# Two feed-forward layers, most gate/value products by Strassen's seven-product block form, the second matrix in four rounds

## The chip, the cores and the metric

The kernel runs on one core of a Trainium2 chip. The metric is device time in microseconds (us) from launch to the last output; smaller is better. Before the change three runs took 1251.07, 1249.19 and 1251.08 us, so the median is 1251.07.

The engines are named as in the profile: PE multiplies matrices, PEld loads its weights, DVE, ACT and POOL work elementwise, SP issues the transfers (DMA). Sums of products are formed in PSUM, everything else is kept in SBUF, both with 128 partitions.

## The reference

The trunk has two layers over 512 tokens of 1024 channels. Each layer is a mixer (layer 0: gated short convolution and attention; layer 1: a convolution module) and then a SwiGLU feed-forward, each between two norms and added to the stream. The change is in the feed-forward and in the norm behind it:

```python
def rms_norm(x, g):
    y = xf * lax.rsqrt(jnp.mean(xf * xf, axis=-1, keepdims=True) + RMS_EPS)
    return y * g
def swiglu_ffn(h, w_ffn_in, w_ffn_out):
    g, u = jnp.split(h @ w_ffn_in, 2, axis=-1)      # (512,1024) @ (1024, 2*2816)
    return (jax.nn.silu(g) * u) @ w_ffn_out         # (512,2816) @ (2816,1024)
...
for layer in range(2):
    ...                                             # mixer
    f = swiglu_ffn(rms_norm(h, norm_ffn_pre[layer]), w_ffn_in[layer], w_ffn_out[layer])
    h = h + rms_norm(f, norm_ffn_post[layer])
```

## The kernel before

Channels lie on partitions, tokens on the free axis: a tile is 128 channels by 512 tokens, and the stream is `NK` = 8 such tiles. Every float32 product is carried by three passes over operands that are split as v = H + L (`mm3`, lines 188 to 193: `wh` by `xh`, `wh` by `xl`, `wl` by `xh`). A weight block is 128 by 128, and 8 of them make one chunk of 512 KB. `ensure` streams the chunks in the order in which they are used: SP loads one into a raw buffer (`wr`, 2 of them), ACT copies it, rounded, into `wh` (line 173), DVE subtracts that from the raw chunk into `wl` (line 175; POOL for a few chunks outside the feed-forward). `wh` and `wl` have 5 buffers each. `take` asks for two chunks beyond the one in use.

The inner dimension 2816 of the feed-forward is 22 tiles. One *pair* is the gate tile and the value tile of the same 128 inner channels: 2 x 8 blocks x 3 passes = 48 matmuls of 512 columns (`pairs`). `glu_evict` then takes both sums out of PSUM: DVE multiplies each by `R`, the per-token factor of the norm (lines 783, 785), ACT does the Silu of the gate (784), DVE multiplies the two (786), and the result is split by ACT (`gh`, 787) and DVE (`gl`, 788). It lies in numbered slots `z`.

Each feed-forward is done in two halves of 11 pairs. Pairs 0 and 1 of the first are made in `cross`, in token halves, while the norm ahead is still being finished. After pairs 2 to 10 the first half's second product follows: `rows` makes 8 output tiles (`m`) of 11 k steps each, 33 matmuls of 512 columns a tile. Six of these partial sums go to SBUF (`KEPT`), the two others are put back into PSUM later by matmuls with an identity (lines 718 to 720). Then come pairs 11 to 21 and the second half's product: `WIDE` = 5 whole tiles, and the last three in token halves (`half_rows`), so that the norm behind them can begin on one half. `Boundary` adds the partial sums, normalises and adds to the stream.

PE runs its instructions in the order in which the program writes them. For DVE, ACT, POOL and SP a scheduler lays out the order when the program is built; each engine then works strictly along its own queue, so an instruction that has to wait holds up all that are queued behind it.

## Time and profile before

| | before |
|---|---|
| median of three runs, us | 1251.07 (1249.19 to 1251.08) |
| span of the profiled execution, us | 1248.6 |
| PE busy, us (share of the span) | 1185.8 (95%) |
| weight loads on PE, us | 1005.8 (81%) |
| DVE busy, us | 735.6 (59%) |
| ACT busy, us | 490.0 (39%) |
| POOL busy, us | 265.0 (21%) |
| mean granted TensorE clock (1.00 is full speed) | 0.978 |

The profiled execution is listed with its span alone, from the first to the last instruction, 2.5 us under the median of the runs. Shares are means over the whole span. The two feed-forwards are stages of their own in it (about 243 to 655 us and 842 to 1230 us), in which the engines are used quite differently from the rest; the profile's table of 40 slices and its windows show that. Idle time of an engine is listed with its releaser, the event that ended it.

### The profile page before, as it was taken

Reading aid. Unit: us, or ns where it says so; the run is one execution under the profiler, and the core shown is the slowest. Engines: PE = TensorE matmul, PEld = TensorE weight load, DVE = VectorE, ACT = ScalarE, POOL = GpSimd, SP = SyncE. Lnnn points to the kernel's source line nnn. Section 1 sums busy time; section 2 is a strip of 40 time slices with the busy share of each in tenths; the row PEclk is TensorE's granted clock in tenths of the full one; section 3 lists DMA queues with packets and bytes.
Section 4 is the critical chain, followed back from the end, with each engine's and each line's share of the span. In section 5 each row is a group of like instructions: output and inputs, shape, how many; then the busy total and the mean of one; then the engine's idle time right before and its main releaser. Section 6 shows DMA issues by size and latency. Waiting matters only on the chain.

```text
span 1248.6 us, 15995 instructions
## 1 busy us (share of the span) xinstructions
PE 1185.8 (95%) x6134; PEld 1005.8 (81%) x6134; DVE 735.6 (59%) x1266; ACT 490.0 (39%) x862; POOL 265.0 (21%) x268
## 2 busy tenths in 40 slices
PE   8899999989999999999988998898999999999996
PEld 6677677888888888888887897898888888888885
DVE  7578985496443234443398999948844422444425
ACT  4366664534332222332244575464332322332220
POOL 4132322460000000001475359124300000000021
PEclk9999999999999999999989999898999999999998
DMA  5332223313233233223221543123133233233212
GB/s 177 113 106 85 85 68 102 119 51 99 89 100 102 87 99 101 94 92 102 92 71 52 168 131 97 28 68 102 51 101 101 88 98 99 89 101 102 90 46 68
DMA packets 43116, 115.86 MB, mean 93 GB/s; under 512 B 4696, under 2 KB 14040, under 8 KB 43040
## 3 DMA queue, kind: packets, MB, share of 16 engines
q1 hardware_dynamic: 39936, 109.30, 28.1%
q10 hardware_dynamic: 2384, 3.15, 0.8%
q0 software_dynamic: 720, 2.39, 0.6%
q8 instruction: 48, 0.79, 0.3%
q14 instruction: 28, 0.23, 0.1%
HBM read 109.05 MB, written 5.78 MB: 92 GB/s over the span
## 4 chain that ended last, share of the span: by engine, by line
PE 73%; DVE 17%; DMA 4%; ACT 2%; issue 2%; POOL 1%; SPq 0%; ACTq 0%; DVEq 0%; POOLq 0%
PE pg L191 22%; PE pg L193 22%; PE pg L192 22%; DVE xl L675 2%; DVE h L672 2%; DVE wl L175 2%; DVE tb L663 2%; PE pg L737 1%; DVE st_u L281 1%; POOL acc L234 1%; PE ps L298 1%; PE pg L734 1%; DMA wr<-w_fi 1%; PE pg L735 1%; PE pp L541 1%
## 5 line engine op out<-in xcount | busy, mean ns | idle before, releaser
L191 PE MATMUL pg<-xh,wh 128*128 128x512 f32 (+1 forms) x960 | 372.1, 388 | 0.2 <-DVE z L459 0.2
L193 PE MATMUL pg<-xh,wl 128*128 128x512 f32 (+1 forms) x960 | 368.4, 384 | 2.0 <-DVE wl L175 2.0
L192 PE MATMUL pg<-xl,wh 128*128 128x512 f32 (+1 forms) x960 | 367.8, 383 | 2.0 <-DVE xl L331 2.0
L173 ACT ACTIVATE wh<-wr 128x1024 fp32r<-128x1024 f32 (+1 forms) x186 | 193.3, 1040 | 424.3 <-PE pg L192 349.9
L175 DVE TENSOR_TENSOR wl<-wr,wh 128x1024 fp32r<-128x1024 f32 (+1 forms) x157 | 192.3, 1226 | 168.2 <-ACT wh L173 168.1
L234 POOL TENSOR_TENSOR acc<-acc,sq 128x256 f32<-128x256 f32 x70 | 63.7, 925 | 749.5 <-ACT sq L241 746.5
L193 PEld LDWEIGHTS pg<-xh,wl 128*128 128x128 f32 x960 | 181.1, 189 | 38.8 <-DVE wl L175 3.0
L192 PEld LDWEIGHTS pg<-xl,wh 128*128 128x128 f32 x960 | 181.4, 189 | 36.6 <-DVE xl L331 2.8
L191 PEld LDWEIGHTS pg<-xh,wh 128*128 128x128 f32 x960 | 181.6, 189 | 33.9 <-issue 0.7
L191 PE MATMUL pg<-z,wh 128*128 128x512 f32 (+1 forms) x514 | 183.2, 357 | 0.0
L192 PE MATMUL pg<-z,wh 128*128 128x512 f32 (+1 forms) x514 | 182.1, 354 | 1.1 <-DVE z L391 1.1
L193 PE MATMUL pg<-z,wl 128*128 128x512 f32 (+1 forms) x514 | 182.1, 354 | 0.0
L192 PEld LDWEIGHTS pg<-z,wh 128*128 128x128 f32 x514 | 97.9, 190 | 15.9 <-DVE z L391 1.5
L191 PEld LDWEIGHTS pg<-z,wh 128*128 128x128 f32 x514 | 97.9, 190 | 14.7 <-ACT m L651 0.3
L193 PEld LDWEIGHTS pg<-z,wl 128*128 128x128 f32 x514 | 97.9, 190 | 14.4
L785 DVE TENSOR_TENSOR t<-pg,R 128x512 f32<-128x512 f32 (+1 forms) x48 | 31.0, 645 | 126.9 <-PE pg L193 126.7
L175 POOL TENSOR_TENSOR wl<-wr,wh 128x1024 fp32r<-128x1024 f32 x29 | 71.8, 2476 | 125.4 <-ACT wh L173 113.8
L783 DVE TENSOR_TENSOR t<-pg,R 128x512 f32<-128x512 f32 (+1 forms) x48 | 31.0, 646 | 86.7 <-PE pg L193 83.0
L918 DVE SCALAR_TENSOR_TENSOR ps<-z,vecs,ps 128x512 f32<-128x512 f32 x69 | 47.7, 747 | 0.1
L674 ACT ACTIVATE xh<-h,vecs 128x256 fp32r<-128x256 f32 x48 | 23.4, 506 | 58.4 <-DVE h L672 58.4
L734 PE MATMUL pg<-xh,wh 128*128 128x256 f32 x160 | 44.9, 305 | 1.2 <-ACT xh L1082 1.2
L735 PE MATMUL pg<-xh,wl 128*128 128x256 f32 x160 | 44.3, 301 | 0.0
(250 smaller groups left out, 1526.2 us busy)
## 6 DMA issues: line engine op xcount, KB each, us to landing
wr<-w_fi SPq DMA_DIRECT2D x88, 512.0 KB
wr<-w_fo SPq DMA_DIRECT2D x44, 512.0 KB
wr<-w_p SPq DMA_DIRECT2D x24, 512.0 KB
wr<-w_in SPq DMA_DIRECT2D x16, 512.0 KB
wr<-w_out SPq DMA_DIRECT2D x8, 512.0 KB
h<-x SPq DMA_DIRECT2D x8, 256.0 KB
wr<-w_xa SPq DMA_DIRECT2D x8, 256.0 KB
wr<-w_v SPq DMA_DIRECT2D x4, 512.0 KB
```

What stands on the lines that cost most here:

```text
L173: act(h[:, cs], raw[:, cs], AF.Copy)
L175: eng.tensor_tensor(out=l[:, cs], in0=raw[:, cs], in1=h[:, cs], op=ALU.subtract)
L191: mm(ps, wh, xh, start=first, stop=False)
L192: mm(ps, wh, xl, start=False, stop=False)
L193: mm(ps, wl, xh, start=False, stop=last)
L234: eng.tensor_tensor(out=acc, in0=acc, in1=t, op=ALU.add)
L663: stt(out=t, in0=self.s[k][:, cs], scalar=col(self.gpost + k), in1=rp, op0=ALU.mult, op1=ALU.mult)
L734: mm(ps, wh, xt[0][k][:, cs], start=k == 0 and m % 2 == 0, stop=False)
L735: mm(ps, wl, xt[0][k][:, cs], start=False, stop=False)
L783: tt(out=tg, in0=pg, in1=R[:, cs], op=ALU.mult)
L785: tt(out=tu, in0=pu, in1=R[:, cs], op=ALU.mult)
L918: stt(out=a if j < n - 1 else res, in0=u[:, j : j + T], scalar=w_col(i, j), in1=a, op0=ALU.mult, op1=ALU.add)
```

## The change

Of each feed-forward's 22 pairs, 0 to 3 stay as they are (`CLASSIC`). Pairs 4 to 21 are made by Strassen's form in Winograd's variant. The pair is read as a 2x2 block product: the gate matrix over the value matrix, each cut into two halves of the 1024 input channels (`a11 a12` over `a21 a22`), times the tokens' input, cut into channel halves and token halves (`b11 b12` over `b21 b22`). Seven products replace eight; each has 4 k steps x 3 passes of 256 columns. For them

- `combine` loads both weight chunks and builds `s1`, `s3`, `s2` (POOL) and `s4` (DVE) from them, and splits seven quarter-pair blocks into 4 + 4 buffers; the last split's subtract is POOL's;
- `strassen_x` and `strassen_last` build sums `t1` to `t4` of the tokens' input once a layer, on POOL, DVE and ACT;
- `strassen` runs the seven products, takes each out of PSUM and puts the sums together: ACT copies two, DVE combines five of 256 columns, POOL makes two steps of 512 (`tu` and the product with `R`).

The 22 inner tiles are worked in four rounds of 5, 6, 5, 6 pairs (`ROUNDS`), each followed by its part of the second product into 8 partial sums in SBUF: the first round copies them there, the others add to them on DVE. `WIDE` goes from 5 to 2, and the identity matmuls go. The second matrix's chunks are cut across output tiles, with 2 or 3 DMAs each, and are split by ACT and DVE. The value side isn't multiplied by `R` any more; the norm behind the feed-forward gets an epsilon per token for that.

The diff, cut to its core (line numbers in the text on the changed kernel are those of the changed file):

```diff
+ROUNDS = ((0, 5), (5, 11), (11, 16), (16, 22))
+CLASSIC = 4
-WIDE = 5
-KEPT = 6
+WIDE = 2
...
         def add_ffn(l):
-            for hf in range(2):
-                for i in range(HALF):
-                    for s in range(2):
-                        add("fi", w_fi[:, l, hf * HALF + i, s], s if (hf, i) == (0, 0) else None)
-                for c in range(HALF):
-                    add("fo", w_fo[:, l, hf, c])
+            for p0, p1 in ROUNDS:
+                for p in range(p0, p1):
...
+                        add("fs", (w_fi[:, l, p, 0], w_fi[:, l, p, 1]))
...
+                for c in range(n):
...
+                    add("fo", parts)
...
+                if name == "fo":
+                    r3 = raw.rearrange("p (a b) -> p a b", a=8)
+                    for lo, hi, part in ap:
+                        nc.sync.dma_start(r3[:, lo:hi], part)
+                    act(h, raw, AF.Copy)
+                    tt(out=l, in0=raw, in1=h, op=ALU.subtract)
...
+        def combine(top, bottom):
+            i = combined[0]
+            combined[0] += 1
+            a1 = alloc("wr", (P, D), F32, 2)
+            a2 = alloc(("pth", "ptl")[i % 2], (P, 2560), F32)
+            s4 = slot(12 + i % 2, dt=F32)
+            nc.sync.dma_start(a2[:, :D], bottom)
+            nc.sync.dma_start(a1, top)
+            hs, ls = ([alloc(n, (P, D), FR, 5) for _ in range(4)] for n in ("wh", "wl"))
+            pool = nc.gpsimd.tensor_tensor
+
+            def half(i, src, eng=nc.vector):
+                n = src.shape[1]
+                act(hs[i][:, :n], src, AF.Copy)
+                eng.tensor_tensor(out=ls[i][:, :n], in0=src, in1=hs[i][:, :n], op=ALU.subtract)
...
+            pool(out=s1, in0=a2[:, :T], in1=a2[:, T:D], op=ALU.add)
+            half(0, a1)
+            pool(out=s32.rearrange("p (a b) -> p a b", a=2),
+                 in0=a2[:, : 2 * D].rearrange("p (a b) -> p a b", a=2)[:, :, :T],
+                 in1=a1[:, :T].unsqueeze(1).to_broadcast([P, 2, T]), op=ALU.add)
+            half(1, a2[:, T : D + T])
+            half(2, s32)
+            tt(out=s4, in0=s2, in1=a1[:, T:], op=ALU.add)
+            half(3, s4, nc.gpsimd)
...
+        def strassen_x(bd, gpre):
...
+                pool(out=t1, in0=a[:, HT:], in1=a[:, :HT], op=ALU.subtract)
+                tt(out=t2, in0=b[:, HT:], in1=t1, op=ALU.subtract)
...
+        def strassen(xs, R, g, p):
+            w = take("fs", 1)[0]
+            def product(a, b):
+                ps = psum("g")[:, :HT]
+                for j in range(4):
+                    js = slice(j * P, (j + 1) * P)
+                    mm3(ps, (w[a][0][:, js], w[a][1][:, js]), xs[j][b], j == 0, j == 3)
+                return ps
...
+            act(p1, product("a11", "b11"), AF.Copy)
+            act(p5, product("s1", "t1"), AF.Copy)
+            tt(out=u23[:, lo], in0=product("s2", "t2"), in1=p1, op=ALU.subtract)
+            tt(out=tg[:, lo], in0=product("a12", "b21"), in1=p1, op=ALU.add)
+            tt(out=u23[:, hi], in0=product("s3", "t3"), in1=u23[:, lo], op=ALU.add)
+            nc.gpsimd.tensor_tensor(out=tu.rearrange("p (a b) -> p a b", a=2),
+                                    in0=u23.rearrange("p (a b) -> p a b", a=2),
+                                    in1=p5.unsqueeze(1).to_broadcast([P, 2, HT]), op=ALU.add)
+            tt(out=tg[:, hi], in0=product("s4", "b22"), in1=tu[:, lo], op=ALU.subtract)
+            nc.gpsimd.tensor_tensor(out=tg, in0=tg, in1=R, op=ALU.mult)
+            act(tg, tg, AF.Silu)
+            tt(out=tu[:, lo], in0=product("a22", "t4"), in1=u23[:, hi], op=ALU.add)
+            tt(out=tu, in0=tu, in1=tg, op=ALU.mult)
+            act(gh, tu, AF.Copy)
+            tt(out=gl, in0=tu, in1=gh, op=ALU.subtract)
...
+            def more(m, ps, c0, cn):
+                tt(out=part[m], in0=ps, in1=part[m], op=ALU.add)
+
+            for r, (p0, p1) in enumerate(ROUNDS):
+                weave(chain(*(strassen(xs, pre.R, g, p) for p in range(max(p0, CLASSIC), p1))))
+                st, rhs = Stream("fo"), [g[i][1:] for i in range(p1 - p0)]
+                if r < len(ROUNDS) - 1:
+                    weave(rows(st, p1 - p0, rhs, range(NK), more if r else first))
```

What that does to the queues is seen at three places. Names carry a buffer number; `z` slots hold `gh` and `gl`, `sq` and `sqp` the first two products, `acc` the pair of sums `u23`, `pth` and `ptl` the value chunk and its sums, in turn.

DVE's queue in the middle of a half, one pair before the change:

```order
L783 TENSOR_TENSOR t_653_3139<-pg_646_3081,R_490_2060 128x512
L175 TENSOR_TENSOR wl_661_3180<-wr_659_3178,wh_660_3179 128x1024
L785 TENSOR_TENSOR t_654_3140<-pg_650_3112,R_490_2060 128x512
L786 TENSOR_TENSOR t_654_3140<-t_654_3140,t_653_3139 128x512
L175 TENSOR_TENSOR wl_669_3221<-wr_667_3219,wh_668_3220 128x1024
L788 TENSOR_TENSOR z11_652_3138<-t_654_3140,z10_651_3137 128x512
```

The same engine after, one pair in the middle of the second round:

```order
L913 TENSOR_TENSOR acc_812_3838<-pg_817_3869,sq_813_3839 128x256
L929 TENSOR_TENSOR z5_784_3700<-t_786_3702,z4_783_3699 128x512
L915 TENSOR_TENSOR t_810_3836<-pg_818_3883,sq_813_3839 128x256
L218 TENSOR_TENSOR wl_805_3820<-ptl_798_3811,wh_801_3816 128x1024
L917 TENSOR_TENSOR acc_812_3838<-pg_819_3897,acc_812_3838 128x256
L229 TENSOR_TENSOR z12_824_3947<-pth_823_3946,wr_822_3945 128x512
L218 TENSOR_TENSOR wl_806_3821<-ptl_798_3811,wh_802_3817 128x1024
L922 TENSOR_TENSOR t_810_3836<-pg_820_3912,t_811_3837 128x256
L926 TENSOR_TENSOR t_811_3837<-pg_821_3928,acc_812_3838 128x256
L218 TENSOR_TENSOR wl_829_3954<-wr_822_3945,wh_825_3950 128x1024
L927 TENSOR_TENSOR t_811_3837<-t_811_3837,t_810_3836 128x512
```

Six instructions have become eleven: three weight splits instead of two, one sum of weights (229), and five evictions of 256 columns for two of 512.

POOL's queue before has nothing between the last square of the norm ahead of the first feed-forward and the sums of the norm behind it:

```order
L234 TENSOR_TENSOR acc_526_2338<-acc_526_2338,sqp_570_2624 128x256
L247 TENSOR_TENSOR sqp_572_2632<-h6_464_2026 128x256
L247 TENSOR_TENSOR sqp_574_2640<-h7_465_2027 128x256
L234 TENSOR_TENSOR acc_526_2338<-acc_526_2338,sqp_572_2632 128x256
L234 TENSOR_TENSOR acc_924_4723<-acc_924_4723,sq_929_4767 128x256
```

After, there are five instructions for each of the 18 pairs; for the pair shown above they are

```order
L222 TENSOR_TENSOR pth_823_3946<-pth_823_3946 128x512
L224 TENSOR_TENSOR pth_823_3946<-pth_823_3946,wr_822_3945 128x1024
L918 TENSOR_TENSOR t_811_3837<-acc_812_3838,sqp_814_3840 128x512
L218 TENSOR_TENSOR wl_807_3822<-z13_799_3812,wh_803_3818 128x512
L923 TENSOR_TENSOR t_810_3836<-t_810_3836,R_490_2060 128x512
```

The first two already work for the pair after the next (`pth_823`), the fourth for the next one (`wl_807`).

ACT's queue where the first half's pairs end and the second product begins, before:

```order
L784 ACTIVATE t_713_3499<-t_713_3499 128x512
L173 ACTIVATE wh_734_3581<-wr_733_3580 128x1024
L787 ACTIVATE z20_711_3497<-t_714_3500 128x512
L173 ACTIVATE wh_738_3613<-wr_737_3612 128x1024
L802 ACTIVATE m0_715_3507<-pg_725_3517 128x512
```

The same engine where the second round ends, after:

```order
L928 ACTIVATE z8_833_3969<-t_836_3972 128x512
L185 ACTIVATE wh_866_4200<-wr_865_4199 128x1024
L185 ACTIVATE wh_869_4207<-wr_868_4206 128x1024
L185 ACTIVATE wh_873_4240<-wr_872_4239 128x1024
L924 ACTIVATE t_852_4089<-t_852_4089 128x512
L185 ACTIVATE wh_877_4273<-wr_876_4272 128x1024
L928 ACTIVATE z10_850_4087<-t_853_4090 128x512
```

Before, the last pair's Silu (784) has one chunk of the second matrix between itself and `gh` (787). Now three chunks (185) stand ahead of the last pair's Silu (924) and a fourth between it and `gh` (928).

## Rows read from the trace of the kernel before

**Rows 1.** The page: POOL's busy time, and its tenths in 40 slices of the span.

```profile
PE 1185.8 (95%) x6134; PEld 1005.8 (81%) x6134; DVE 735.6 (59%) x1266; ACT 490.0 (39%) x862; POOL 265.0 (21%) x268
...
POOL 4132322460000000001475359124300000000021
```

**Rows 2.** Windows (from:to length, busy us by engine, clock, DMA share, GB/s).

```profile
core 0: us, PE busy (x) PEld busy (x) DVE busy (x) ACT busy (x) POOL busy (x), PEclk, DMA share, GB/s
300.00:430.00 130.00, 130.00 (x569) 106.52 (x568) 51.28 (x58) 39.10 (x47) 0.00 (x0) 1.00 0.31 97
```

**Rows 3.** Timeline of PE (start, length of one) in a pair, 26 steps apart.

```profile
319.83 0.39 PE L192 MATMUL pg<-xl,wh 128*128 128x512 f32 x1
...
325.73 0.39 PE L191 MATMUL pg<-xh,wh 128*128 128x512 f32 x1
```

**Rows 4.** Timeline of PE in second products: 31 steps, then 55 of 256 columns.

```profile
395.70 0.40 PE L192 MATMUL pg<-z,wh 128*128 128x512 f32 x1
...
402.95 0.39 PE L193 MATMUL pg<-z,wl 128*128 128x512 f32 x1
...
1209.31 0.28 PE L191 MATMUL pg<-z,wh 128*128 128x256 f32 x1
...
1215.85 0.28 PE L192 MATMUL pg<-z,wh 128*128 128x256 f32 x1
```

**Rows 5.** Timeline of DVE: the same instruction in two pairs that follow each other.

```profile
355.85 0.69 DVE L783 TENSOR_TENSOR t<-pg,R 128x512 f32<-128x512 f32 x1 [2.22 <-PE pg L193]
...
366.73 0.69 DVE L783 TENSOR_TENSOR t<-pg,R 128x512 f32<-128x512 f32 x1 [2.21 <-PE pg L193]
```

**Rows 6.** Groups by form (busy us, mean ns of one, idle before and releasers).

```profile
L175 DVE TENSOR_TENSOR wl<-wr,wh 128x1024 fp32r<-128x1024 f32 x149 | 185.8, 1248 | 168.2 <-ACT wh L173 168.1
L788 DVE TENSOR_TENSOR z<-t,z 128x512 fp32r<-128x512 f32 x40 | 27.4, 685 | 0.7 <-ACT z L787 0.7
L783 DVE TENSOR_TENSOR t<-pg,R 128x256 f32<-128x256 f32 x8 | 3.4, 419 | 3.7 <-ACT R L683 3.6
L173 ACT ACTIVATE wh<-wr 128x1024 fp32r<-128x1024 f32 x178 | 188.4, 1059 | 424.2 <-PE pg L192 349.9 <-issue 34.5 <-DMA wr<-w_v 11.1
L784 ACT ACTIVATE t<-t 128x512 f32<-128x512 f32 x40 | 25.3, 632 | 0.1
L175 POOL TENSOR_TENSOR wl<-wr,wh 128x1024 fp32r<-128x1024 f32 x29 | 71.8, 2476 | 125.4 <-ACT wh L173 113.8 <-DVE ps L918 7.0 <-PE pp L256 4.6
L881 POOL TENSOR_TENSOR z<-z,z 128x512 f32<-128x512 f32 x15 | 17.7, 1202 | 0.0
```

**Rows 7.** Timeline of POOL and DVE where both work at once.

```profile
160.83 2.40 POOL L175 TENSOR_TENSOR wl<-wr,wh 128x1024 fp32r<-128x1024 f32 x1 [7.71 <-ACT wh L173]
160.98 0.35 DVE L524 SCALAR_TENSOR_TENSOR h<-h,ccol,ps 128x128 f32<-128x128 f32 x1 [0.17 <-PE ps L520]
...
161.50 2.27 DVE L388 TENSOR_TENSOR t<-t,m 128x512 f32<-128x512 f32 x1
...
243.99 1.22 DVE L175 TENSOR_TENSOR wl<-wr,wh 128x1024 fp32r<-128x1024 f32 x1 [1.41 <-ACT wh L173]
...
244.31 1.51 POOL L234 TENSOR_TENSOR acc<-acc,sq 128x256 f32<-128x256 f32 x1 [8.48 <-ACT sq L241]
...
253.00 0.92 POOL L234 TENSOR_TENSOR acc<-acc,sq 128x256 f32<-128x256 f32 x1
253.24 1.76 DVE L175 TENSOR_TENSOR wl<-wr,wh 128x1024 fp32r<-128x1024 f32 x1
```

**Rows 8.** The chain of waits: transfers of whole chunks on it (start, length).

```profile
830.05 5.05 DMA wr<-w_p
...
837.47 3.42 DMA wr<-w_fi
```

**Rows 9.** Windows after a wait of PE (columns as in the second group).

```profile
664.00:667.00 3.00, 0.00 (x0) 0.00 (x0) 2.89 (x8) 0.00 (x0) 2.55 (x4) 1.00 0.00 0
667.00:670.00 3.00, 2.80 (x13) 2.80 (x14) 1.24 (x4) 1.52 (x2) 0.00 (x0) 0.52 0.00 0
670.00:673.00 3.00, 3.00 (x19) 2.76 (x19) 1.89 (x4) 2.46 (x7) 1.36 (x1) 0.91 0.00 0
```

More of the change, by code (lines that the diff above doesn't have):

```diff
@@ L157, in ensure @@
                 name, ap, spare = chunks[len(split)]
+                if name == "fs":
+                    split.append((name, combine(*ap), None))
+                    continue
                 count[name] = count.get(name, -1) + 1
@@ L289, in rsqrt_cols @@
             b = alloc("st_b", (P, 4), F32, 3)[:, :n]
+            if not isinstance(eps, float):
+                stt(out=a, in0=sums, scalar=scale, in1=eps, op0=ALU.mult, op1=ALU.add)
+                ts(out=b, in0=a, scalar1=-0.5, scalar2=None, op0=ALU.mult)
+                return newton(a, b, n)
             ts(out=a, in0=sums, scalar1=scale, scalar2=eps, op0=ALU.mult, op1=ALU.add)
@@ L627, in trunk, with __init__ @@
         class Boundary:
[L630 removed]
+            def __init__(self, gpost, gpre, bias=None, kept=(), before=None):
+                self.before, self.eps = before, {}
                 self.gpost, self.gpre, self.bias = gpost, gpre, bias
@@ L653, in post0 @@
             def post0(self, hf):
-                self.cols[hf] = rsqrt_cols(self.sums.cols(hf), 2, 1.0 / D, RMS_EPS)
+                eps = RMS_EPS if self.before is None else self.before.eps[hf]
+                self.cols[hf] = rsqrt_cols(self.sums.cols(hf), 2, 1.0 / D, eps)
             def post1(self, hf):
@@ L679, in pre0 @@
             def pre0(self, hf):
-                self.cols[hf] = rsqrt_cols(self.pre.cols(hf), 2, 1.0 / D, RMS_EPS)
+                sums = self.pre.cols(hf)
+                self.cols[hf] = rsqrt_cols(sums, 2, 1.0 / D, RMS_EPS)
+                self.eps[hf] = alloc(f"st_eps{hf}", (P, 4), F32)[:, :2]
+                ts(out=self.eps[hf], in0=sums, scalar1=RMS_EPS / D, scalar2=RMS_EPS * RMS_EPS, op0=ALU.mult, op1=ALU.add)
             def pre1(self, hf):
@@ L707, in rows, with half_rows @@
                     yield
-        def half_rows(st, nk, rhs, ms, hf, evict, base=0, back={}):
+        def half_rows(st, nk, rhs, ms, hf, evict, base=0):
             cs = slice(hf * HT, (hf + 1) * HT)
@@ L715, in half_rows @@
                     mm3(ps, st[(m - base) * nk + k], (rhs[k][0][:, cs], rhs[k][1][:, cs]),
-                        k == 0, k == nk - 1 and m not in back)
+                        k == 0, k == nk - 1)
                     if k == nk - 1:
-                        if m in back:
-                            for j in range(2):
-                                mm(ps, eye, back[m][j][:, cs], start=False, stop=j == 1)
                         evict(m, ps, hf * HT, HT)
@@ L772, in cross, with glu_room @@
             return [(LATE0[n], bd.steps("pre0", 1)), (LATE1[n], lambda: ready(1))]
+        def glu_room(g, p):
+            i = p - max(r[0] for r in ROUNDS if r[0] <= p)
+            if i not in g or g[i][0] != p:
+                g[i] = (p, slot(2 * i), slot(2 * i + 1))
+            return g[i][1:]
         def glu_evict(g):
@@ L792, in ffn @@
         def ffn(pre, g, late, gpost, gpre):
             evict = glu_evict(g)
-            weave(pairs("fi", pre, 2, HALF, evict), late)
-            part = {m: alloc(f"m{m}") for m in range(KEPT)}
-            back = {m: (slot(22 + 2 * i), slot(23 + 2 * i)) for i, m in enumerate(range(KEPT, NK))}
-            def keep(m, ps, c0, cn):
-                if m < KEPT:
-                    act(part[m], ps, AF.Copy)
-                else:
-                    act(back[m][0], ps, AF.Copy)
-                    tt(out=back[m][1], in0=ps, in1=back[m][0], op=ALU.subtract)
@@ L807, in ffn, with first @@
-            weave(rows(Stream("fo"), HALF, [g[i][1:] for i in range(HALF)], range(NK), keep))
-            weave(pairs("fi", pre, HALF, NF, evict))
-            bd = Boundary(gpost, gpre, kept=part.values())
+            xs = []
+            weave(pairs("fi", pre, 2, CLASSIC, evict), late + [(late[-1][0], lambda: xs.extend(strassen_x(pre, pre.gpre)))])
+            strassen_last(pre, xs)
+            part = {m: alloc(f"m{m}") for m in range(NK)}
+            def first(m, ps, c0, cn):
+                act(part[m], ps, AF.Copy)
@@ new lines, in more @@
+            def more(m, ps, c0, cn):
[5 more added lines that the diff above has]
+                    weave(rows(st, p1 - p0, rhs, range(NK), more if r else first))
+            bd = Boundary(gpost, gpre, kept=part.values(), before=pre)
@@ L811, in done @@
             def done(m, ps, c0, cn):
-                bd.evict(m, ps, c0, cn, part.get(m))
-            st, rhs = Stream("fo"), [g[i][1:] for i in range(HALF)]
-            weave(rows(st, HALF, rhs, range(WIDE), done))
-            return bd, lambda hf: half_rows(st, HALF, rhs, range(WIDE, NK), hf, done, 0, back)
+                bd.evict(m, ps, c0, cn, part[m])
+            weave(rows(st, p1 - p0, rhs, range(WIDE), done))
+            return bd, lambda hf: half_rows(st, p1 - p0, rhs, range(WIDE, NK), hf, done)
```

62 lines of the change are left out of this document (56 added, 6 removed).

## The prediction, made before the changed kernel was run

> **What bounds the kernel now.** I read the page's busy shares first, then windows inside a feed-forward, then timelines of PE and DVE there, and last the groups for the price of each operation. Over the whole span PE is busy 95%, and POOL 21% [rows 1]; POOL's slices are empty from the tenth to the eighteenth, so its work lies in the mixers and at the norms. In a stretch of 130 us in the middle of the first feed-forward PE is busy for all of it at clock 1.00 (the 2.4 GHz level), DVE for 51, ACT for 39, POOL not at all, DMA 0.31 [rows 2]. There PE alone sets the time, and fewer columns would be time gained as long as the others keep up. DVE does the same instruction 10.88 us later in the next pair (355.85 to 366.73), each time after 2.2 us of waiting for PE [rows 5]: one pair costs 10.88.
>
> What a column costs: 26 steps of 512 columns take 5.90 us, 0.2269 each [rows 3], so 48 make 10.89, which agrees. In the second product 31 steps take 7.25, 0.2339 each; 55 steps of 256 columns take 6.54, 0.1189 each [rows 4]. A 256-column step is therefore a little more than half of one of 512.
>
> **The change part by part.**
>
> *A. Seven products for eight.* A pair becomes 7 x 4 x 3 = 84 steps of 256: 84 x 0.1189 = 9.99 us for 10.89, so 0.90 less. 36 pairs (18 in each layer): **-32.5**. If 256 columns cost just half of 512 (0.1134) it would be 9.53 and -49; at 0.125 it would be 10.50 and -14.
>
> The Trainium skill, "TensorE: Matmul & The Clock Gate", section "Back-to-back issue gap", gives 262 cycles for 256 columns and 518 for 512 at full clock, an isolated gap. As an estimate from that page a pair would go from 10.36 to 9.17, and A would be -42.8. The trace's 118.9 and 226.9 ns are longer than those 109.2 and 215.8, so the trace decides.
>
> *B. Identity matmuls.* 16 steps of 256 go in the two layers: 16 x 0.1189 = **-1.9**.
>
> *C. The port between DVE and POOL in the middle of a round.* The trace shows one thing that the busy shares hide. Where DVE and POOL both read two operands from SBUF, one waits for the other. A POOL operation ends at 253.92, and a DVE split that had started at 253.24 ends at 255.00, 1.08 after it and not 1.2 after its own start; a 512-column DVE operation ends 0.54 after the end of a POOL split (163.23 to 163.77); and the other way round a POOL sum of 256 ends 0.61 after a DVE split's end at 245.21 [rows 7]. A DVE operation with a PSUM operand takes its usual 0.35 in the middle of a POOL split [rows 7]. So I read the two engines' SBUF work as one resource: DVE holds it 1.08 for 1024 columns and 0.54 for 512. For POOL I take 1.17 for 512 and 2.27 for 1024, a shade under the means of 1.20 and 2.48, which contain waits [rows 6].
>
> Before, POOL has no work in the pairs. After, a pair has on DVE three splits of 1024 and three operations of 512 with both inputs in SBUF (s4, the product of gate and value, `gl`): 3 x 1.08 + 3 x 0.54 = 4.86. POOL has s1, `tu`, the fourth split and the product with `R`, 4 x 1.17, and s3 with s2, 2.27: 6.95. Together 11.81, over PE's 9.99. I then walked the four queues through a pair in their order, with ACT 1.06 for a chunk's copy and 0.63 for 512 [rows 6]. The resource isn't always passed on at once: two evictions (0.42 each [rows 6]) and a start lie between holders, about 1.0, so a full pair takes 12.8. The first pairs of a round have their weight sums made ahead, while the second product runs, so the walk gives 9.99, 9.99, 11.14, 12.79, 12.79, 10.94 in a round of six and 9.99, 9.99, 11.14, 12.79, 10.94 in one of five: 7.7 and 4.9 above PE's pace. The first round has one such pair and no excess. A layer has 7.7 + 4.9 + 7.7 = 20.3, two layers **+40.6**. Ends: 15, if the work made ahead reaches further and the gaps close; 45, if POOL takes its means of 2.48 and 1.20. Below nothing neither this nor D, E or F can go, since they are waits on top of PE's pace, which A has.
>
> *D. The start of a second product.* Its last k step needs `gl` of the round's last pair. Before, that came 10 k steps, 30 x 0.2339 = 7.0 us, into the row, which covered the chain of evictions. Now it is 4 or 5 k steps: by the third pass, 13 steps (3.04 us) or 16 (3.74). The last pair's Silu stands behind three chunks of the second matrix on ACT's queue, and `gh` behind a fourth; with two raw buffers the fourth chunk's load waits for the second chunk's split on DVE. Counted from the end of PE's last product: that split ends about 0.5; the load takes 4.2, the middle of 3.42 and 5.05 [rows 8], to 4.7; ACT's copy to 5.7; Silu to 6.3; DVE's split to 7.0 and the product to 7.6; `gh` to 8.25; DVE's next split to 8.7; `gl` to 9.4. PE waits 6.3 in rounds of five, 5.6 in rounds of six: 4 x (6.3 + 5.6) = **+47.6**. With no port and loads of 3.42 `gl` comes at about 6.4, and the waits are 3.4 and 2.7: 24. With loads of 5.05 it is 54.
>
> *E. The clock after such a wait.* Where PE had done nothing from 664 to 667, its next 3 us ran at 0.52 and the 3 after at 0.91 [rows 9]: 0.48 x 3 + 0.09 x 3 = 1.7 us lost. Eight waits: **+13.7**, between 0, if these waits are too short for a fall of the clock, and 27, if it falls for twice as long.
>
> *F. Token sums.* `t1` to `t4` are made on POOL and DVE in the two classic pairs (2 x 10.9 us) after the norm; 3 x 4 POOL steps of 256 at 0.61, 4 of their splits on DVE, and the first Strassen pair wants the last at its seventh product. I take 2 a layer: **+4**, 0 to 10.
>
> *At nothing.* The new adds of partial sums are 16 a layer on DVE, 0.69 each, one to a row of 3.5 us or more on PE; without that cover they would be 22. The extra DMA pieces are SP's alone. `WIDE` 2 doubles a step's count for three more tiles (2 x 0.1189 against 0.2339: 0.004 x 3 x 18 x 2, 0.4). The epsilon is one small operation at a norm. The dropped product with `R` is DVE's, which waits for PE before.
>
> Sum: -32.5 - 1.9 + 40.6 + 47.6 + 13.7 + 4 = +71.5 on the profiled span 1248.6, that is 1320; the median of the runs is 2.5 above the span, so **1322**.
>
> **The rivals.**
>
> *R1. The port doesn't bind within the pairs.* If the weight sums run far enough ahead that POOL's and DVE's work fits into the shadow of evictions, C falls away, and of D 30 stays (4 x (4.1 + 3.4), `gl` at 7.1 without the port). -34.4 + 30 + 13.7 + 4 = +13.3: **1264**. For it: DVE and POOL together hold the port 11.81, and POOL's first two steps already work two pairs ahead. Against it: 11.81 over 9.99 is more than a reordering can hide in rounds of 5 and 6.
>
> *R2. Faster: PE stays the bound.* Here the port costs nothing measurable, and the second product's start is covered, because the chunks land earlier than the walk says and the wait is too short to touch the clock. What is left are A and B, -34.4, and F with some 10 of residual waits: **1227**. The point from which it decides: C, D, E and F together have to stay under 34.4, less than half of what I have for C and D. For it: DMA has a share of 0.31 in the pairs [rows 2], DVE and ACT 51 and 39 of 130, so by busy time alone all fits. Against it: the order of ACT's queue at a round's end, and rows 7.
>
> *R3. Seven eighths aren't delivered.* Weight loads come with half as many columns to hide them. The 256-column rows show 0.1189 [rows 4], but in a stage where DVE and DMA do less. At 0.125 A is -14 and the sum **1341**.
>
> **How the numbers follow.** The forecast (port and round starts, 1290 to 1348): 0.62. R1, 1250 to 1290: 0.16. R2, up to 1248: 0.16. R3, which overlaps the forecast's upper part: 0.06. 0.2% is 2.5 us, about what a measurement of this kernel can tell from no change. Faster by more than that takes nearly all of R2: 0.16; within it lies the seam of R1 and R2: 0.03; slower: 0.81. For the range I go down to 1238, which takes in R1 and the upper part of R2, and up to 1348, the sum with C, D and E near their upper ends for two of the three; 0.2 stays out.
>
> **What the profile after would show.** Between DVE's evictions of the third product (line 913) about 10 us in a round's first two pairs and 12.8 from the fourth: C right; 10 throughout: R1 or R2. The mean of DVE's splits (218) well over 1.25: the port. PE idle some 6 us, ended by DVE's `gl` (929), at each of eight second products, and the clock under 1.00 in the stretch behind: D and E; one or two us with the clock at 1.00: R2. PE steps of 256 at 0.119 where nothing waits: A; 0.125: R3. POOL's share over 21% in any case. The forecast is wrong above all if DVE and POOL get along with two SBUF operands each, or if the fourth chunk's load starts well before the last product's end.

## The result

The changed kernel takes 1344.12 us (median of four runs, 1342.46 to 1345.06), the kernel before 1251.07: 1.0732 times as long, 95% interval 1.0708 to 1.0757 (estimated from all runs, the kernel before's now four, up to 1256.14, so not quite the quotient of the medians). The forecast was 1322, the range 1238 to 1348. The profiled execution has a span of 1342.1 for 1248.6, so 93.5 us are to be found.

The page of the changed kernel (as [rows 1], with the granted clock by slices):

```profile
PE 1191.0 (89%) x7432; PEld 1060.6 (79%) x7432; DVE 922.7 (69%) x1514; ACT 585.0 (44%) x1038; POOL 625.6 (47%) x472
...
POOL 3132233545276265275475468026624743734732
PEclk9899999898999899999889999798989989989988
```

PE is busy about as long as before (1191.0 for 1185.8), but 89% of a longer span; POOL went from 21% to 47%, and the clock dips in places. What PE waited for is told by the view of its waits (engine and line of the waiting instruction, what it waited for: us in total, times, longest), of which these are the five lines of the feed-forward:

```profile
PE pg L247 <- ACT z L928: 36.5, 8, 5.9
PE pg L247 <- DVE t L922: 24.7, 20, 1.5
...
PE pg L247 <- DVE t L851: 9.4, 2, 6.1
...
PE pg L247 <- DVE t L915: 6.4, 10, 1.0
PE pg L248 <- DVE z L929: 4.7, 8, 0.8
```

Eight waits for `gh` (928) and eight for `gl` (929) are the eight round starts. The waits for lines 922 and 915, up to 1.5 us, are PSUM tiles that come back late within the pairs and lengthen them. The two for line 851 are one in each layer, where the first Strassen pair begins.

**Pairs.** DVE and POOL in a full pair of the second round (timeline: start, length):

```profile
391.00 0.41 DVE L913 TENSOR_TENSOR acc<-pg,sq 128x256 f32<-128x256 f32 x1
391.77 2.12 DVE L929 TENSOR_TENSOR z<-t,z 128x512 fp32r<-128x512 f32 x1 [0.36 <-ACT z L928]
...
396.22 2.32 DVE L218 TENSOR_TENSOR wl<-pth,wh 128x1024 fp32r<-128x1024 f32 x1
...
403.98 0.41 DVE L913 TENSOR_TENSOR acc<-pg,sq 128x256 f32<-128x256 f32 x1
```

```profile
390.61 2.74 POOL L224 TENSOR_TENSOR ptl<-ptl,wr 128x1024 f32<-128x1024 f32 x1
395.84 1.61 POOL L918 TENSOR_TENSOR t<-acc,sqp 128x512 f32<-128x512 f32 x1 [2.49 <-DVE acc L917]
```

The two evictions of the third product are 12.98 apart. `gl` takes 2.12 us in place of the 0.69 of [rows 6]: it ends at 393.89, 0.54 after POOL's sum at 393.35. The split that takes 2.32 ends at 398.54, 1.09 after POOL's step at 397.45. These are the amounts of [rows 7]. Over all pairs the same split (line 218, on the value chunk) takes 1401 ns in the mean, and 1218 in the kernel without POOL's steps that follows below; `gl` takes 1326 and 682:

```profile
L218 DVE TENSOR_TENSOR wl<-pth,wh 128x1024 fp32r<-128x1024 f32 x36 | 50.4, 1401 | 5.0 <-ACT wh L217 5.0
L929 DVE TENSOR_TENSOR z<-t,z 128x512 fp32r<-128x512 f32 x36 | 47.7, 1326 | 10.2 <-ACT z L928 10.2
```

```profile
L218 DVE TENSOR_TENSOR wl<-pth,wh 128x1024 fp32r<-128x1024 f32 x36 | 43.9, 1218 | 7.3 <-ACT wh L217 7.3
L929 DVE TENSOR_TENSOR z<-t,z 128x512 fp32r<-128x512 f32 x36 | 24.6, 682 | 0.0
```

**Round starts.** Windows over the second round's pairs and over the second product behind them (columns as in [rows 2]), then over four stretches of that product's beginning:

```profile
362.27:430.22 67.95, 61.69 (x506) 60.50 (x505) 48.94 (x58) 30.44 (x46) 43.53 (x23) 1.00 0.30 86
430.22:472.06 41.84, 36.64 (x146) 28.73 (x145) 20.50 (x23) 8.93 (x10) 12.26 (x7) 0.92 0.30 88
...
434.00:437.00 3.00, 0.00 (x0) 0.00 (x0) 1.98 (x3) 1.68 (x3) 1.07 (x1) 1.00 0.57 175
437.00:440.00 3.00, 0.92 (x2) 0.42 (x2) 1.93 (x3) 1.47 (x2) 0.00 (x0) 0.65 0.62 175
440.00:443.00 3.00, 3.00 (x7) 2.35 (x8) 0.69 (x1) 0.00 (x0) 0.21 (x1) 0.50 0.60 175
443.00:446.00 3.00, 3.00 (x11) 2.37 (x10) 1.60 (x1) 1.06 (x1) 2.17 (x1) 0.71 0.00 0
```

Six pairs take 67.95, for 6 x 10.02 = 60.1 at PE's pace (84 steps take 10.02 where nothing waits). The product's 144 steps at 0.2339 are 33.68 and take 41.84: PE stands from 433.7 to 438.5, and once more for 1.1, and then runs at 0.50, which is the 1.2 GHz level, until about 445.

The account of all 93.5 us, worked out from PE's timeline. In pairs: time from the first step to the end of the last one, less 10.02 a pair. In second products: gaps at the two waiting steps are waits, what is left over 0.2339 a step is the clock. (The view of waits has 36.5 + 4.7 = 41.2 us for the same waits, since it counts from a step's end and the step between the two waits is itself slow.) At the first Strassen pair: the time from the end of the crossing to the end of that pair, less what the same work takes without waits (98.95 for nine pairs before, less seven at 10.89, plus one at 10.02: 32.74).

| step | forecast | measured |
|---|---|---|
| A. 36 pairs | -32.5 | -31.3 (10.02 for 10.89) |
| B. identity matmuls | -1.9 | -1.9 (taken over, not measured apart) |
| C. six long rounds | +40.6 | +39.6 (7.8, 4.9, 7.3; 7.6, 4.9, 7.1) |
| D. waits at eight round starts | +47.6 | +46.4 (4.2, 5.9, 6.7, 7.1; 4.5, 5.9, 6.4, 5.6) |
| E. clock behind them | +13.7 | +16.3 (1.5 to 2.8 each) |
| F. first Strassen pair | +4 | +18.3 (10.3 and 8.0) |
| outside the feed-forwards | 0 | +5.8 |
| sum | +71.5 | +93.2 |

### The profile page after: what moved, and what is told of

Read it like the earlier page. It is cut to its first block, busy times and chain, and to the rows that moved or that the text cites. A ratio compares the mean times of both kernels' runs of the same rounds, so it can differ in the third digit from the quotient of the medians.

```text
span 1342.1 us, 19606 instructions
## 1 busy us (share of the span) xinstructions
PE 1191.0 (89%) x7432; PEld 1060.6 (79%) x7432; DVE 922.7 (69%) x1514; ACT 585.0 (44%) x1038; POOL 625.6 (47%) x472
## 4 chain that ended last, share of the span: by engine, by line
PE 52%; DVE 25%; POOL 8%; DMA 6%; ACT 5%; issue 5%; SPq 1%; ACTq 0%; DVEq 0%; POOLq 0%
PE pg L248 15%; PE pg L247 15%; PE pg L249 14%; POOL t L918 3%; DMA wr<-w_fo 3%; DVE xl L738 2%; DVE h L735 2%; DVE wl L218 2%; POOL t L923 2%; POOL wl L218 2%; DVE wl L197 1%; DVE tb L726 1%; DVE wl L186 1%; PE pg L798 1%; DVE ps L1059 1%
## 5 line engine op out<-in xcount | busy, mean ns | idle before, releaser
L247 PE MATMUL pg<-z,wh 128*128 128x256 f32 (+1 forms) x952 | 316.9, 333 | 61.5 <-ACT z L928 36.5
L247 PE MATMUL pg<-xh,wh 128*128 128x256 f32 (+1 forms) x960 | 312.8, 326 | 17.0 <-DVE t L851 9.4
L248 PE MATMUL pg<-z,wh 128*128 128x256 f32 (+1 forms) x952 | 312.9, 329 | 5.8 <-DVE z L929 4.7
L249 PE MATMUL pg<-z,wl 128*128 128x256 f32 (+1 forms) x952 | 310.8, 326 | 0.0
L249 PE MATMUL pg<-xh,wl 128*128 128x256 f32 (+1 forms) x960 | 308.1, 321 | 2.0 <-DVE wl L197 2.0
L248 PE MATMUL pg<-xl,wh 128*128 128x256 f32 (+1 forms) x960 | 307.5, 320 | 1.6 <-DVE xl L391 1.6
L247 PEld LDWEIGHTS pg<-z,wh 128*128 128x128 f32 x952 | 185.8, 195 | 84.2 <-ACT z L928 40.0
L248 PEld LDWEIGHTS pg<-z,wh 128*128 128x128 f32 x952 | 185.2, 195 | 24.3 <-DVE z L929 8.4
L249 PEld LDWEIGHTS pg<-z,wl 128*128 128x128 f32 x952 | 185.3, 195 | 15.1
L195 ACT ACTIVATE wh<-wr 128x1024 fp32r<-128x1024 f32 (+1 forms) x70 | 70.6, 1008 | 69.7 <-PE pg L248 27.0
L923 POOL TENSOR_TENSOR t<-t,R 128x512 f32<-128x512 f32 x36 | 73.8, 2051 | 6.2 <-DVE t L922 6.2
L197 DVE TENSOR_TENSOR wl<-wr,wh 128x1024 fp32r<-128x1024 f32 (+1 forms) x41 | 49.2, 1199 | 37.6 <-ACT wh L195 37.5
L927 DVE TENSOR_TENSOR t<-t,t 128x512 f32<-128x512 f32 x36 | 36.9, 1024 | 49.8 <-ACT t L924 49.8
L185 ACT ACTIVATE wh<-wr 128x1024 fp32r<-128x1024 f32 x44 | 46.0, 1053 | 51.1 <-DMA wr<-w_fo 36.5
```

The lines of the kernel that those rows point to most:

```text
L185: act(h, raw, AF.Copy)
L195: act(h[:, cs], raw[:, cs], AF.Copy)
L197: eng.tensor_tensor(out=l[:, cs], in0=raw[:, cs], in1=h[:, cs], op=ALU.subtract)
L247: mm(ps, wh, xh, start=first, stop=False)
L248: mm(ps, wh, xl, start=False, stop=False)
L249: mm(ps, wl, xh, start=False, stop=last)
```

## Experiments

A ratio is to the kernel before, which ran again beside each group of experiments (medians 1251.33, 1251.18 and 1250.51 us); the changed kernel did not, so differences to it are between groups.

**The port (C).** The first kernel takes POOL's five steps of a pair to DVE, the second only one of them.

```diff
-            pool = nc.gpsimd.tensor_tensor            # s1, and s3 with s2
+            pool = nc.vector.tensor_tensor
...
-            half(3, s4, nc.gpsimd)
+            half(3, s4)
...
-            nc.gpsimd.tensor_tensor(out=tu.rearrange("p (a b) -> p a b", a=2),
+            nc.vector.tensor_tensor(out=tu.rearrange("p (a b) -> p a b", a=2),
...
-            nc.gpsimd.tensor_tensor(out=tg, in0=tg, in1=R, op=ALU.mult)
+            tt(out=tg, in0=tg, in1=R, op=ALU.mult)
```

> The five POOL steps of every Strassen pair (two sums of weights, the last split, the two steps of 512 on the outputs) run on DVE; nothing else changes. Theory (DVE and POOL share a port for two SBUF operands, and POOL holds it about twice as long for the same columns): POOL is empty in the pairs, the port is DVE's alone. DVE's own work in a pair rises to about 10.5 us (5 evictions at 0.34, four steps of 1024 at 1.14, seven of 512 at 0.61), a little over PE's 10.0, so the interval between two evictions of the third product falls from 12.8 to 10.5 to 11.0, and the 39.6 us of excess in the six long rounds to 10 to 20. The waits at the eight round starts shorten by about 1 each. Time 1305 to 1320. Rival (the long pairs come from DVE's queue and the length of the chain, not from the port): DVE has half as much again to do, the interval stays at 12.8 or grows, time 1344 or more.

1282.21 us, ratio 1.0254 (1.0223 to 1.0285): 62 us less than the changed kernel, and below the range of either theory. Windows over the second round's pairs, the product behind them, and three of the pairs:

```profile
360.63:420.78 60.15, 60.15 (x506) 60.14 (x505) 53.13 (x81) 32.72 (x46) 0.00 (x0) 1.00 0.32 100
420.78:457.40 36.62, 34.17 (x146) 27.00 (x145) 22.66 (x29) 8.18 (x10) 0.00 (x0) 1.00 0.30 96
...
375.44:405.35 29.91, 29.91 (x253) 29.91 (x252) 28.95 (x45) 16.50 (x23) 0.00 (x0) 1.00 0.29 92
```

Six pairs in 60.15, PE busy for all of it: the excess of the six long rounds is 0.1 in place of 39.6, with DVE busy 97%. So the excess was not a queue too long or work too much on DVE: it came with POOL's part, and the stretched steps above show the turns at the port. How much was POOL's slower steps on the way to the outputs, this kernel alone doesn't tell; the next one moves a step that isn't on that way. I had put DVE's work at 10.5 a pair, and it was 9.65 (28.95 over three). The waits at the round starts fell too, from 46.4 to 31.4.

```diff
-            pool(out=s32.rearrange("p (a b) -> p a b", a=2),
+            tt(out=s32.rearrange("p (a b) -> p a b", a=2),
```

> As the changed kernel, but one of POOL's five steps of a pair, the sum that makes s3 and s2 (1024 columns), runs on DVE; it lies off the chain that leads to the pair's outputs. Theory (the two engines' time at the port adds up): it holds the port 1.08 there for 2.27, so a full pair's interval falls from 12.8 to about 11.6, the excess of the six long rounds from 39.6 to about 20, and the waits at round starts hardly change: 1322 to 1328. Rival (what counts is that the output chain goes over POOL and back): the interval stays at 12.8, or grows by up to 1.1 with DVE's added work: 1342 to 1375.

1329.31 us (1.0616, 1.0597 to 1.0635), the excess 26.3. The same round:

```profile
361.59:426.51 64.92, 61.47 (x506) 60.42 (x505) 47.90 (x60) 31.88 (x46) 34.72 (x20) 1.00 0.29 90
```

It lost 3.0 us of its 7.8, and its first four intervals between third-product evictions are 11.75 in the mean for 12.50, unevenly (9.38 to 14.18). The rival would have left the round at 67.95, since this step is on no path to the outputs: port time adds up. But the excess fell by 13.3 us and not by the 19.6 that the prices promised, and the total came out 1 us over the range expected; one round (6.4) gained less than its like.

**The round starts (D, E).** In the first kernel ACT's copies of the second matrix's chunks, from a round's second chunk on, wait for the last pair's `gl`; in the next the product begins with three tiles; in the last two PE is kept busy.

```diff
-                    act(h, raw, AF.Copy)
+                    if place and lastgl:               # place: the chunk's number in its round
+                        if place == 1:
+                            lastgl.append(alloc("st_z", (P, 1), F32, 2))
+                            act(lastgl[-1], lastgl[-2][:, :1].bitcast(F32), AF.Copy, scale=0.0)
+                        act(h, raw, AF.Identity, bias=lastgl[-1])
+                    else:
+                        act(h, raw, AF.Copy)
...
+            lastgl.append(gl)
```

> As the changed kernel, but ACT's copies of the second matrix's chunks, from the second chunk of a round on, wait for the last pair's low part (through a bias of zero made from it), so neither they nor their splits stand in front of that pair's steps. Theory (at a round start the pair's steps are held up by these copies and splits in the queues and at the port): without them the low part comes about 3.5 us after PE's last product instead of 9.5, the waits of 4 to 7 us fall to 0 to 1, the clock stays up, 40 to 58 us of the 46.5 + 17 come back: 1286 to 1304. Rival (the pair's own chain is long, or the chunks then come too late): less than 15 us come back, 1330 or more, with PE waiting for a chunk's split instead.

1303.33 us (1.0418, 1.0388 to 1.0449). Waits 14.6 for 46.4, clock 4.9 for 16.3, the long rounds as before (39.2):

```profile
423.60:459.53 35.93, 34.43 (x147) 26.93 (x146) 20.78 (x21) 10.83 (x12) 9.10 (x6) 1.00 0.33 103
```

So 43 us were the chunks in front of the last pair's steps. Which link held them up is not quite what the walk had said. ACT at the end of the second round in the changed kernel:

```profile
430.06 1.06 ACT L185 ACTIVATE wh<-wr 128x1024 fp32r<-128x1024 f32 x1 [0.79 <-DMA wr<-w_fo]
434.18 1.06 ACT L185 ACTIVATE wh<-wr 128x1024 fp32r<-128x1024 f32 x1 [3.06 <-DMA wr<-w_fo]
435.14 0.61 ACT L924 ACTIVATE t<-t 128x512 f32<-128x512 f32 x1
436.90 1.06 ACT L185 ACTIVATE wh<-wr 128x1024 fp32r<-128x1024 f32 x1 [1.14 <-DMA wr<-w_fo]
437.86 0.61 ACT L928 ACTIVATE z<-t 128x512 fp32r<-128x512 f32 x1
```

The late chunk is there as forecast (4.0 us after PE's last product at 430.2; 4.7 was expected), and the Silu stands behind its copy. But POOL's product with `R`, which the Silu also needs, ended at 435.08, no sooner: a DVE split that a POOL step had stretched to 2.23 us had held up the eviction ahead of it (922; timeline of POOL and DVE):

```profile
431.01 1.30 POOL L918 TENSOR_TENSOR t<-acc,sqp 128x512 f32<-128x512 f32 x1 [3.90 <-DVE acc L917]
431.16 2.23 DVE L186 TENSOR_TENSOR wl<-wr,wh 128x1024 fp32r<-128x1024 f32 x1 [0.29 <-ACT wh L185]
433.31 0.41 DVE L922 TENSOR_TENSOR t<-pg,t 128x256 f32<-128x256 f32 x1
433.81 1.27 POOL L923 TENSOR_TENSOR t<-t,R 128x512 f32<-128x512 f32 x1 [1.50 <-DVE t L922]
```

Two delays of the same length lay side by side, and the walk had named one. With the chunks out of the way `gl` came 5.5 after the last product, not 3.5.

```diff
...
+            todo = [(m, k) for m in first for k in range(nk - 1)] + [(m, nk - 1) for m in first]
+            todo += [(m, k) for m in ms[len(first):] for k in range(nk)]
+            for m, k in todo:                          # first: three tiles, two in the last round
...
```

> As the changed kernel, but each second product begins with three output tiles together (two in a layer's last round): all their k steps but the last, then the three last ones. PE then has 8.4 us of work in a round of five and 10.5 in one of six (7.0 in the last) before it needs the last pair's low part, for 2.8 to 3.5. Theory (the wait is a matter of what PE has to do before that part is there, some 9 to 10 us after its last product): waits fall from 46.5 to under 10 us in all, and the 16 us of slow clock behind them to 0 to 5, while the long pairs stay at 12.8: 1285 to 1300. Rival (the second matrix's chunks then come too late, or tiles wait for PSUM): PE waits for a chunk's split instead, 1320 or more.

1301.77 us (1.0407, 1.0379 to 1.0434). The waits at the round starts are 8.2 in all and the clock 1.2; the long rounds stay (38.2). The product that took 41.84 now takes

```profile
423.15:456.81 33.66, 33.66 (x147) 27.09 (x145) 16.49 (x22) 8.08 (x10) 11.06 (x7) 1.00 0.36 110
```

PE's pace, and no wait for a chunk. The total is 1.8 us above the range expected, because the edit did one thing more: its new constant took the name of the one (`FIRST`) that says how many channel tiles give the mean of layer 1's convolution, and PE waited 12.6 us there.

```diff
...
+                    if st.name == "fo" and m == ms[0] and k == nk - 1:
+                        for j in range(FILL):          # 7; nought is a weight block of zeros, plain float32
+                            mm(ps, nought.bitcast(F32), rhs[0][0].bitcast(F32), start=False, stop=False)
```

> Seven products of 512 columns with a weight block of zeros are added ahead of the last k step of the first tile of each of the eight second products, where PE waits for the last pair; they add nothing to the sum and take some 5 to 6 us by the spacing of plain float32 products elsewhere in the kernel. Theory (17 us of the loss are the clock, which falls because PE stands still for 4 to 7 us): the granted clock stays at 1.00 behind the round starts, 17 us come back, 3 to 4 are lost where the added products are longer than the wait: about 1330. Rival (the slow 4 to 6 us behind a wait are not from PE's idleness): the clock falls as before and the time is 1344 to 1350.

> The kernel of e3_fill with its new constant under a name of its own (there it had taken the place of the one that paces the attention of layer 0, which cost some 27 us ahead of the first feed-forward). Theory (16 us of the loss are the clock, which falls because PE stands still): as there the clock stays at 1.00 at the eight round starts, 16 us come back, 4 are lost where the added products are longer than the wait, and the attention is as in the changed kernel: 1332, 1328 to 1337. Rival (what the rounds gained there was lost elsewhere for the same reason): 1344 or more.

The first of these took 1355.88 us, since its constant took the name of the one that paces layer 0's attention; the first feed-forward began 29 us late, and the total tells nothing. The second, with that mended, took 1327.49 (1.0621, 1.0604 to 1.0638), 17 us less than the changed kernel and 0.5 under the range expected, with seven products more at each of eight places; 12.6 of the 17 lie at the round starts. The second round's product in it:

```profile
428.44:468.09 39.65, 39.65 (x160) 29.74 (x159) 17.48 (x23) 8.06 (x10) 13.11 (x7) 1.00 0.30 93
```

The added products take as long as the wait did (50.0 in all for 46.4), the clock stays at 1.00, and behind them nothing is lost (0.1 for 16.3). In both kernels the steps behind the wait are the same and only PE's standing still differs, so E is the clock, and it comes from PE's idleness.

**The rounds alone.**

```diff
-CLASSIC = 4
+CLASSIC = 22
...
-                weave(chain(*(strassen(xs, pre.R, g, p) for p in range(max(p0, CLASSIC), p1))))
+                weave(pairs("fi", pre, max(p0, 2), p1, evict), () if r else late)
```

> All 22 pairs are made as before the change, in the four rounds and with all the rest of the change; no Strassen pair and none of its sums of weights and tokens. Theory (rounds cost little by themselves; the wait at a round start comes from the Strassen pair, whose seven products end together and whose steps share the port and the queue with the splits): the last pair needs only the value's product, a copy and a subtract, so PE waits 0 to 1 us per round, time 1250 to 1262. Rival (the rounds themselves cost it, since the second matrix comes through two raw buffers and is needed sooner): waits of 3 us and more with a lower clock behind them, 1280 to 1310.

1254.67 us, 1.0022 (1.0008 to 1.0035). The second round's pairs and the product behind them:

```profile
351.32:416.54 65.22, 65.22 (x289) 53.98 (x288) 25.32 (x28) 19.40 (x24) 0.00 (x0) 1.00 0.31 97
416.54:450.31 33.77, 33.77 (x147) 27.16 (x146) 13.30 (x15) 7.00 (x8) 0.00 (x0) 1.00 0.29 94
```

PE never waits at a round start, though the rounds, the chunks and the raw buffers are the same. A classic pair needs three short steps behind its last product; a Strassen pair's outputs all come together at its end. The 3 us over the kernel before lie outside the rounds (in the profiled executions 4.6 more ahead of the first of them and 2.6 less between the layers) and were not followed.

**The first Strassen pair (F).**

```diff
-                pool = nc.gpsimd.tensor_tensor         # t1, t3, t4 of the token sums
+                pool = nc.vector.tensor_tensor
```

> As the changed kernel, but the twelve steps a layer by which POOL builds the token sums run on DVE. Theory (the wait of 6.1 and 3.3 us ahead of the first Strassen pair, and that pair's slow start, come from DVE and POOL taking turns at the port, since the classic pairs' evictions stand behind the sums on DVE): the wait falls to under 2 a layer, 8 to 12 us in all come back: 1332 to 1336. Rival (it is DVE's queue that is too long there, whoever shares the port): DVE has twelve more steps of 0.34 in front of the evictions, the wait grows by 2 to 4 a layer, 1346 to 1352.

1333.04 us (1.0645, 1.0629 to 1.0661), 11 us less. The stretch from the crossing to the end of the first Strassen pair in layer 0, before the change (nine classic pairs), in the changed kernel and in this one:

```profile
283.79:382.74 98.95, 98.95 (x443) 82.04 (x442) 50.93 (x77) 33.38 (x46) 0.00 (x0) 1.00 0.32 101
```

```profile
285.41:328.49 43.08, 36.21 (x191) 31.70 (x190) 35.08 (x57) 24.18 (x44) 20.22 (x18) 0.88 0.23 64
```

```profile
286.76:326.98 40.22, 36.04 (x192) 31.24 (x191) 34.75 (x69) 23.72 (x44) 8.76 (x6) 0.92 0.23 69
```

32.74 would be free of waits. DVE does twelve steps more and PE waits less: here too the port is a part. But 7.5 and 6.4 us of the 10.3 and 8.0 stay. POOL still has some steps of the weights in this kernel; in f3 below it has none in this stretch, and 7.4 and 3.9 stay there, 11 of the 18 us without any turn at the port. Those are the rival's: DVE's queue. What stood on it ahead of the classic pair's eviction (851), and PE's wait for that, in the changed kernel (timeline of DVE, then of PE):

```profile
308.25 1.53 DVE L891 TENSOR_TENSOR xl<-m,xh 128x256 fp32r<-128x256 f32 x1
309.70 1.21 DVE L877 TENSOR_TENSOR z<-acc,z 128x512 fp32r<-128x512 f32 x1
310.83 0.94 DVE L879 TENSOR_TENSOR z<-m,z 128x256 fp32r<-128x256 f32 x1
311.69 0.94 DVE L871 TENSOR_TENSOR acc<-t,acc 128x256 f32<-128x256 f32 x1
312.56 1.21 DVE L186 TENSOR_TENSOR wl<-wr,wh 128x1024 fp32r<-128x1024 f32 x1
313.69 1.21 DVE L877 TENSOR_TENSOR z<-acc,z 128x512 fp32r<-128x512 f32 x1
314.82 0.68 DVE L851 TENSOR_TENSOR t<-pg,R 128x512 f32<-128x512 f32 x1
...
315.65 0.55 PE L247 MATMUL pg<-xh,wh 128*128 128x256 f32 x1 [6.11 <-DVE t L851]
```

The other 7 us of the gain lie elsewhere, 3 of them between the layers, where this edit changes nothing; so the total fits the theory's range partly by luck.

**Together.** f1 has POOL's five steps on DVE, the three tiles and the token sums on DVE in one, f1b the same with `FIRST` left as it was; f3 adds to it that DVE makes the four band products that POOL makes at the boundary between the layers; f4 adds a fifth classic pair to f3.

```diff
-BUILD = ('PPPPPDPP', 'PPAPDDPA', 'APPPADDD', ...)     # f3
+BUILD = ('DDDPPDPP', 'PPAPDDPA', 'APPDADDD', ...)
-CLASSIC = 4                                           # f4
+CLASSIC = 5
```

> All three together: the pairs' five POOL steps on DVE, the token sums on DVE, and second products that begin with three tiles. Theory: pairs at PE's pace of 10.0 (as with the first of them alone, 1282), and of that kernel's 31 us of waits at round starts and 14 of slow clock behind them, and some 8 at the first Strassen pairs, all but 10 come back: 1225 to 1245, faster than before the change by 0.5 to 2%. Rival (DVE is now busy all the time, 97% in a pair in the first of these kernels, so whatever is gained at one place is waited for at the next): 1255 to 1282.

> The kernel of f1 with its new constant under a name of its own (there it had taken the place of the one that says how many channel tiles of layer 1's convolution give the mean, 3 for 1, and PE waited 13 us for their sums). Theory (both feed-forwards run at PE's pace already, and the rest of f1's shortfall is this wait and the one at the boundary between the layers): 12 to 14 us less than f1's 1248, that is 1234 to 1238. Rival (the tap products behind that wait are late anyway): 1243 to 1249.

> As f1b, but the four band products that POOL makes at the boundary between the layers (5.6 us in a row, in front of the last sums of squares that PE waits 10.7 us for) are DVE's. Theory (POOL's queue sets that wait): it falls to 3 to 6, time 1228 to 1233. Rival (it is DVE's queue or the norm's chain): no gain, 1234 to 1240.

> As f3, but five classic pairs a layer, not four, so the first round has no Strassen pair and the token sums have a whole second product more of time. Theory (the wait ahead of the first Strassen pair, 3.9 us in f1 in layer 0 and 1 in layer 1, is for evictions that stand behind the token sums): it goes, and a classic pair costs 0.87 a layer more: 2 to 4 us less than f3. Rival (the evictions of the classic pairs wait as before, with the second product behind them): same as f3 or up to 2 more.

f1 took 1248.44 us (0.9971, 0.9959 to 0.9984): both feed-forwards ran at PE's pace, but it lies 3 above the range expected, for most of the gain was lost at the wait for the mean. f1b took 1233.57 (0.9865, 0.9848 to 0.9881), 0.4 under the theory's range. f3 took 1235.31 (0.9886, 0.9865 to 0.9906), no faster than f1b: PE's wait at the boundary, here of f1b and of f3, hardly moved, so the band products in POOL's queue don't set it; what does is open.

```profile
637.98 0.56 PE L313 MATMUL pp<-ones,acc 128*128 128x1 f32 x2 [10.16 <-DVE acc L291]
```

```profile
636.60 0.34 PE L313 MATMUL pp<-ones,acc 128*128 128x1 f32 x1 [8.81 <-DVE acc L291]
```

f4 took 1223.73 us, 0.9791 (0.9770 to 0.9812): 2.1% faster than the kernel before, the fastest of all. It gained 12 us on f3 where 2 to 4 were expected. Up to the end of the classic pairs it is 2.6 and 0.3 us over a pace without waits, where f3 was 7.4 and 3.9 over at its first Strassen pair; less 1.7 for two classic pairs more that explains 7. The other 5 lie ahead of the first feed-forward (1.5), in the token halves at its end (1.6) and between the layers (1.6), where the edit changes nothing. Its second round:

```profile
347.78:407.92 60.14, 60.14 (x505) 60.14 (x504) 53.13 (x81) 32.72 (x46) 0.00 (x0) 1.00 0.32 100
407.92:441.58 33.66, 33.66 (x146) 27.09 (x145) 22.13 (x29) 7.97 (x10) 0.00 (x0) 1.00 0.32 105
```

## Why the prediction was right, and where it was off

- **What bounded the kernel** was read rightly: PE alone, in the feed-forward. The change moved the bound to a resource that no busy share shows, and to waits at which PE stands.
- **The range** held the result, 1344 under 1348, partly by luck. Its upper end was given as the sum with two of C, D and E near their upper ends; by their figures any two make at most 1342, and all three 1346.
- **A** was off by 1.2: a pair takes 10.02, 0.1193 a step, for the 0.1189 of [rows 4]. The estimate from the Trainium skill's "TensorE: Matmul & The Clock Gate", section "Back-to-back issue gap" (109.2 ns), isn't borne out: 119 ns is what every pair without waits shows, in f4 too.
- **C** was right in size and cause: 39.6 for 40.6, a round of six 7.8 for 7.7, one of five 4.9 for 4.9. PE's pairs in the second round take 10.01, 10.03, 11.98, 12.97, 11.94 and 11.02 where the walk had 9.99, 9.99, 11.14, 12.79, 12.79 and 10.94. DVE falls behind one pair before PE does (11.41, 12.77, 12.98, 12.85 and 10.75 between evictions of the third product), so the sign that was named, about 10 in a round's first two pairs, was wrong. R1, which let the port hide, is out; so is R3, with 10.02 a pair. The Trainium skill, "SBUF — State Buffer", section "Who interferes with whom", has this as an exclusive lock between DVE's second port and GpSimd; the collisions above and the kernel without POOL steps agree.
- **D** was right in size (46.4 for 47.6), with a cause that was half named: chunks in front of the last pair's steps, 32 of the 46 us, but by a DVE split at the port as much as by ACT's copy. At the second round's end `gh` came 8.25 us after PE's last product and `gl` 9.6, for 8.25 and 9.4 in the walk; PE's longer wait is for `gh`, not for `gl` as the forecast had said. R2 had asked for that cover to be there; the kernel with three tiles shows what it would have taken.
- **E** was 16.3 for 13.7. The row that it rested on showed 1.7 a wait; the eight lost 1.5 to 2.8.
- **F is the step that failed**: 18.3 for 4, outside its range of 0 to 10, and two thirds of the 22 us by which the forecast fell short. I priced the first Strassen pair's wait for its last token sum, at its seventh product. PE waited at its first, for a PSUM tile of a classic pair, whose eviction (line 851) stood on DVE's queue behind the token sums, 6.1 us in layer 0 and 3.3 in layer 1. Which instructions were queued behind the new ones on DVE was the question that I had asked of the middle pairs and not of this place; and the clock fell there too (0.88 over the stretch), which I had counted for the round starts alone.
- **Nothing outside the feed-forwards** was forecast to move; 5.8 us did, 4.0 of them between the layers, where PE's wait for the last sums of squares grew from 3.3 to 9.2. The kernel with the rounds alone has that wait too (9.2), so it isn't the Strassen pairs'. Nor does it by itself make the 4.0: in that kernel the stretch between the layers takes 255.2, for 257.7 before and 261.8 in the changed kernel, and in the other kernels that leave it as it was it lies between. What moves it is open.

## To carry to other kernels

Before work is given to an engine that looks idle, ask what it shares with the one that it is to relieve: add up how long each holds the shared port in a cycle, and compare that sum, not the busy shares, with the pace of the engine that bounds. Here moving the idle engine's work onto the busy one, to 97%, gained 62 us. And where a product's last input comes out of a long chain, give the bounding engine other tiles to begin before it shortens the chain: that one reordering covered 38 of 46 us of waits, and the clock behind them came back unasked.

## What the hardware showed

DVE can be busy 28.95 of 29.91 us, in three pairs on end, without PE waiting for it once. A 512-column step with both inputs in SBUF took 2.12 us on DVE beside a 1024-column step of POOL, three times its length alone. And a wait of PE can cost more than its length: 5.9 us of waiting at one round start cost another 2.25 in slow steps. Which waits do that can't be read from their length: in the kernel without POOL steps one round start with 2.87 us of waiting lost 0.07 behind it, and another, with 2.95, lost 2.88.
